# Mixer attention of a two-layer trunk: keys' 1/rms rows kept in four groups of 32 partitions and spread in two rounds

## The chip, the core and the metric

The kernel runs on one core of a Trainium2 chip. The metric is the device time of one execution in microseconds (us), the median of several runs. Engines are named as in the profile: PE (TensorE, matmuls), PEld (its weight loads), DVE (VectorE), ACT (ScalarE), POOL (GpSimd) and SP (SyncE, which issues most DMAs).

## The reference, cut to what matters

Two layers, each a mixer block and a sparse expert block, on 272 tokens (16 meta tokens and 256) of width 1024. The mixer runs a gated convolution and an attention of 8 heads beside each other, and merges them by gates. Of the attention, this part matters here:

```
k = jnp.concatenate([k_nope, k_r], axis=-1)     # 8 heads, 64 + 32 wide
q = _rmsnorm(q, q_norm_g)
k = _rmsnorm(k, k_norm_g)                       # k * rsqrt(mean(k*k) + eps) * g, per token and head
...
s = jnp.einsum('bqhd,bkhd->bhqk', qs, k) * scale
...
p = jax.nn.softmax(s, axis=-1)
```

Each head's keys are divided by their own root mean square, one number per token and head: 8 rows of 272 numbers.

## The kernel before, in words

Everything is fp32, with features on partitions and tokens along the free dimension. `hT` holds the hidden state as 8 tiles of 128 features by 272 tokens. A matmul with a weight tile of 1024 by 128 is eight accumulated matmuls of 128 by 128 by 272: `ztile` takes the next weight tile from a ring of four 1 MB buffers (`wraw`, filled by SP), multiplies it with `xg` and leaves the sum in one of three PSUM buffers `z`. In the second layer only 256 tokens are needed from the gates on, so those tiles have 256 columns.

The order of the work is written out by hand. The mixer is a loop over weight tiles: first the projections to queries and keys, then four pairs of tiles for the convolution input (`za`, `zb`), then 16 gate tiles. `attention()` is a generator, and the loops call it a step at a time, so that its small matmuls stand between the tiles' on PE. Each `yield` ends a step. A pair of convolution tiles has four steps (two behind `za`, two behind `zb`) and a gate tile has two. Between the steps, `taps()` puts convolution taps on DVE (`conv`) and on ACT and POOL (`conv2`).

The keys' norm goes like this. Sums of squares of all heads are collected in one PSUM tile, combined into `ss`, and transposed to tokens on partitions (`pt`, L403). DVE copies 16 numbers a token into `xr` (8 for queries, 8 for keys) and takes 1/rms into `rr` by three Newton steps (`rsqrt_steps`, L168 to L173). Two steps later PE transposes the keys' 8 columns back into 8 rows (`pk`, L419), and ACT copies them to `rk` (a tile of the name `mq`). Two steps later still, each head's row is spread over all 128 partitions by a matmul with a selector `seln[:, h]` (8 by 128, ones in row h), into one of the five PSUM banks of the name `aps`. DVE multiplies the head's keys by it (`kh`, L427). Four heads make one step, the other four the next. Scores, softmax, transposes and the mix with the values follow, one stage a weight tile; their PSUM tiles come from the same five banks `aps`.

At the start of a layer, DVE builds `seln` from the identity matrix (L243), clears the edge of `upad` and makes `gqk`. All matmuls go through the helper `mm` at L56, so the profile tells them apart by the tiles' names: `z<-xg,wraw` is a weight tile, `aps<-mq,seln` a spread.

Of the kernel before, what the change touches and what calls it, by code (L numbers as in the profile page):

```python
# [7 lines left out]
F32 = mybir.dt.float32  # L8
# [4 lines left out]
AF = mybir.ActivationFunctionType  # L13
# [7 lines left out]
T = 272  # L21
NH = 8
# [25 lines left out]
def trunk_kernel(ctx: ExitStack, tc: tile.TileContext, a: dict, out: bass.AP, dbg=None, stop=None):  # L48
    nc = tc.nc
    V, S, G, PE = nc.vector, nc.scalar, nc.gpsimd, nc.tensor  # L50
# [4 lines left out]
    def mm(o, l, r, start, stop):  # L55
        PE.matmul(o, l, r, start=start, stop=stop, skip_group_check=True)  # L56
# [57 lines left out]
    ident = pp.tile([128, 128], F32, name="ident")  # L114
# [36 lines left out]
    def rsqrt(pool, x, shape, y):  # L151
        run_all(rsqrt_steps(pool, x, shape, y))
        return y

    def run_all(g):
        for _ in g:
            pass

    def rsqrt_steps(pool, x, shape, y):

        w = pool.tile([128, T], F32, name="rq_w")
        n = 1
        for s_ in shape[1:]:
            n *= s_
        w = w[:, :n]
        if len(shape) == 3:
            w = w.rearrange("p (a b) -> p a b", a=shape[1])
        V.tensor_scalar(w.bitcast(I32), x.bitcast(I32), 1, None, op0=OP.logical_shift_right)  # L168
        V.tensor_scalar(y.bitcast(I32), w.bitcast(I32), -1.0, float(0x5f3759df), op0=OP.mult, op1=OP.add)
        for _ in range(3):  # L170
            V.scalar_tensor_tensor(w, y, -0.5, y, op0=OP.mult, op1=OP.mult)
            V.tensor_tensor(w, w, x, op=OP.mult)  # L172
            V.scalar_tensor_tensor(y, w, 1.5, y, op0=OP.add, op1=OP.mult)  # L173
            yield
# [8 lines left out]
    def square(sq, c, c0):  # L183

        S.activation(sq[:, c, c0:], hT[:, c, c0:], AF.Square)
        if c:
            V.tensor_add(sq[:, 0, c0:], sq[:, 0, c0:], sq[:, c, c0:])

    carry = None
    for l in range(NL):  # L190
# [22 lines left out]
        def big(tag, shape, dt=F32):  # L213
            t_ = mp.tile([128, 8 * T], F32, name=tag, tag=tag)
            n = 1
            for s_ in shape:
                n *= s_
            v_ = t_[:, :n]
            if dt != F32:
                v_ = v_.bitcast(dt)  # L220
            if len(shape) == 2:
                return v_.rearrange("p (a b) -> p a b", a=shape[0])
            if len(shape) == 3:
                return v_.rearrange("p (a b c) -> p a b c", a=shape[0], b=shape[1])
            return v_
# [4 lines left out]
        wuv = mp.tile([128, 512], F32, name="wuv")  # L230
        qh, kh = pp.tile([128, 8, T], F32, name="xh"), mp.tile([128, 8, T], F32, name="kh")
        rope = mp.tile([128, T], F32, name="rope")
        seln = mp.tile([8, 8, 128], F32, name="seln")
        upad = mp.tile([128, 4, T + KW - 1], F32, name="upad")
        gqk = mp.tile([64, 1], F32, name="gqk")

# [3 lines left out]
            scaled(xg, l, c, C_MIX, 0)  # L240
        for c in range(8):
            square(sq, c, 0)
        V.tensor_copy(seln, ident[0:8, 0:8, None].to_broadcast([8, 8, 128]))  # L243
        V.memset(upad[:, :, 0:KW - 1], 0.0)
        V.tensor_mul(gqk, cl[0:64, C_QN:C_QN + 1], cl[0:64, C_KN:C_KN + 1])
        if carry:
# [1 line left out]
        else:  # L248

            p = zp.tile([128, 512], F32, name="z", bufs=3)  # L250
# [13 lines left out]
        def ztile(c0, x=None):  # L264
            x = xg if x is None else x
            n = T - c0
            w_ = next_w()
            p = zp.tile([128, 512], F32, name="z", bufs=3)
            for c in range(8):
                mm(p[:, :n], w_[:, c * 128:(c + 1) * 128], x[:, c, c0:], c == 0, c == 7)  # L270
            return p[:, :n]
# [20 lines left out]
        def aps():  # L292
            return ap_.tile([128, 512], F32, name="aps", bufs=5)
# [16 lines left out]
        def attention():  # L310
# [8 lines left out]
            mq = mp.tile([128, T], F32, name="mq")  # L319
# [55 lines left out]
            for p in range(4):  # L375
                pk = aps()
# [29 lines left out]
            for i0, i1, n in ((0, 2, 128), (2, 3, 16)):  # L406
# [3 lines left out]
                V.tensor_copy(d_[:, :, 0], s_[:, :, :, 0:2])  # L410
                V.tensor_copy(k_[:, :, 1], s_[:, :, :, 8:10])
            rr = rsqrt(mp, xr, [128, 48], mp.tile([128, 48], F32, name="rr"))
            sc = mp.tile([128, 3, 8], F32, name="sc")
            V.tensor_scalar(sc, rr.rearrange("p (i x) -> p i x", i=3)[:, :, 0:8], SCALE, None, op0=OP.mult)
            yield
            yield
            pk = aps()
            for i, (q0, n) in enumerate(QT):
                PE.transpose(pk[0:8, q0:q0 + n], rr[:n, i * 16 + 8:i * 16 + 16], ident[:n, :n])  # L419
            rk = mp.tile([16, T], F32, name="mq")[0:8]  # L420
            S.activation(rk, pk[0:8, :T], AF.Copy)
            yield
            yield
            for h in range(NH):
                pb = aps()
                mm(pb[:, :T], seln[:, h], rk, True, True)
                V.tensor_mul(kh[0:96, h], kh[0:96, h], pb[0:96, :T])  # L427
                if h == 3:
                    yield
            yield  # L430
            oo = big("sq", [4, T])
            vt["o"] = oo
            PR, TP = {}, {}
# [114 lines left out]
            for x in range(11):  # L548
                p = x // 2
# [128 lines left out]
        V.tensor_mul(zk2[64:128], z[64:128], rs[64:128])  # L678
        V.tensor_add(zkr[64:128], zkr[64:128], zk2[64:128])
        att = attention()  # L680
        cvp = conv2()

# [81 lines left out]
        for i in range(8):  # L764
            p = ztile(t0, xh)
# [651 lines left out]
```

## Time and profile before

| | |
|---|---|
| median of 3 runs | 1758.39 us (1755.1 to 1759.44) |
| profiled execution, its own time | 1755.68 us |
| its span, first to last instruction | 1753.9 us |
| mean granted clock of TensorE | 0.995 |
| DMA | 559.38 MB, mean 319 GB/s |
| spreading matmuls `aps<-mq,seln`, both layers | 32 records, 9.2 us busy |
| keys' transposes (L419), both layers | 6 records |

A matmul in fp32 leaves two records. A row of the timeline gives the start and the length of a run of like instructions, in us from the span's start; in square brackets stands how long the engine sat idle before it and what ended that. PE's matmuls overlap in part, so the time that a run takes of PE's sequence is read from its start to the next run's start. "Granted clock" is the share of full speed at which TensorE was allowed to run, 1.00 being full.

### The profile page before, as it was taken

The page shows a single profiled execution, that of the slowest core. Times are in us where ns is not written, and L with a number is a line of the kernel's source. Part 1 is how long each engine was busy: PE and PEld are TensorE (multiplying, and loading weights), DVE is VectorE, ACT ScalarE, POOL GpSimd, SP SyncE. Part 2 cuts the span into 40 slices and gives each one's busy share as a digit, 9 for nine tenths or more (in the row PEclk, how much of TensorE's full clock was granted, in tenths as well). Part 3 has the DMA queues.
Part 4 walks back from the last instruction along what each step waited for, and adds up shares of the span by engine and source line. Part 5 has one row for each costly group of instructions (what it writes and reads, how often), then busy time and mean ns, then how long its engine had stood idle before and what let it go on. Part 6 is the DMA issues. An engine that isn't in the chain of part 4 may idle for free.

```text
span 1753.9 us, 29518 instructions
## 1 busy us (share of the span) xinstructions
PE 1729.5 (99%) x11611; PEld 1614.6 (92%) x11611; DVE 1108.9 (63%) x2900; ACT 480.9 (27%) x1480; POOL 335.5 (19%) x392
## 2 busy tenths in 40 slices
PE   9999999999999999999999999999999999999998
PEld 7678888999999999999986888899999999999998
DVE  5587369897888644444446883697888885333332
ACT  3443113345544111000024431133355441000000
POOL 0131012222111232232200210112221112212220
PEclk9999999999999999999999999999999999999999
DMA  6223456999999999999962234679999999999995
GB/s 235 73 97 121 168 193 240 384 375 420 420 420 421 420 418 419 421 420 417 417 256 81 92 126 167 222 281 394 372 424 424 423 417 417 397 371 397 398 393 206
DMA packets 80811, 559.38 MB, mean 319 GB/s; under 512 B 9240, under 2 KB 12248, under 8 KB 13208
## 3 DMA queue, kind: packets, MB, share of 16 engines
q1 hardware_dynamic: 49488, 338.54, 49.1%
q0 software_dynamic: 30464, 218.35, 30.5%
q8 instruction: 91, 1.49, 0.3%
q10 hardware_dynamic: 720, 0.60, 0.1%
q14 instruction: 48, 0.39, 0.1%
HBM read 556.18 MB, written 1.05 MB: 318 GB/s over the span
## 4 chain that ended last, share of the span: by engine, by line
PE 72%; DMA 10%; issue 9%; DVE 6%; POOL 2%; ACT 1%; SPq 0%; POOLq 0%; DVEq 0%; ACTq 0%
PE po L56 27%; PE z L56 22%; PE A L56 16%; DMA wraw<-vn 6%; DMA gb<-uv,iww 4%; PE aps L56 4%; POOL gb L1183 2%; PE wp L56 1%; DVE va L1194 1%; DVE gb L1208 1%; PE sc L56 1%; PE xp L56 0%; DMA wraw<-w_in 0%; DVE rq_w L172 0%; DVE ex L907 0%
## 5 line engine op out<-in xcount | busy, mean ns | idle before, releaser
L56 PE MATMUL A<-xh,wraw 128*128 128x160 f32 x3776 | 534.8, 301 | 1.2 <-ACT idxT L821 1.2
L56 PEld LDWEIGHTS A<-xh,wraw 128*128 128x128 f32 x3776 | 517.8, 191 | 1.6 <-issue 1.6
L1208 DVE SCALAR_TENSOR_TENSOR gb<-gb,xr 128x1024 f32<-128x1024 f32 x208 | 254.5, 1224 | 396.1 <-DMA gb<-uv,iww 395.5
L1183 POOL DMA_INDIRECT gb<-uv,iww x208 | 231.2, 1111 | 531.5 <-DVE va L1194 372.2
L56 PE MATMUL z<-xg,wraw 128*128 128x272 f32 (+2 forms) x1408 | 331.6, 393 | 0.2 <-DMA wraw<-w_in 0.2
L56 PEld LDWEIGHTS z<-xg,wraw 128*128 128x128 f32 (+1 forms) x1408 | 261.9, 191 | 55.0 <-issue 8.0
L56 PE MATMUL po<-Xh,wraw 128*128 128x160 f32 x2080 | 287.4, 300 | 3.8 <-DMA wraw<-vn 3.2
L56 PEld LDWEIGHTS po<-Xh,wraw 128*128 128x128 f32 x2080 | 283.2, 190 | 6.9 <-DMA wraw<-vn 5.6
L56 PE MATMUL po<-X,wraw 128*128 128x160 f32 x2016 | 278.4, 301 | 4.8 <-ACT gl L1243 2.5
L56 PEld LDWEIGHTS po<-X,wraw 128*128 128x128 f32 x2016 | 275.8, 191 | 6.8 <-DMA wraw<-vn 3.7
L1194 DVE SCALAR_TENSOR_TENSOR va<-gb,am,va 128x1024 f32<-128x1024 f32 x203 | 260.0, 1281 | 2.8 <-ACT am L1219 2.6
L1218 ACT ACTIVATE am<-am 128x1 f32<-128x1 f32 x208 | 41.3, 199 | 594.1 <-DVE gb L1208 594.0
L1122 ACT ACTIVATE ohA<-ohE,wlo 128x128 f16<-128x128 f16 x320 | 105.2, 429 | 6.3 <-DVE ohE L1119 5.5
L612 POOL TENSOR_TENSOR acc<-acc,cp 128x272 f32<-128x272 f32 (+1 forms) x60 | 50.6, 843 | 241.1 <-ACT cp L611 238.7
L1182 POOL COPY warm<-wraw 1x1 f32<-1x1 f32 x86 | 32.6, 379 | 319.7 <-DMA wraw<-vn 319.7
L604 DVE SCALAR_TENSOR_TENSOR acc<-upad,cols,acc 128x272 f32<-128x272 f32 (+1 forms) x180 | 88.6, 548 | 0.2
L1219 ACT ACTIVATE am<-am,iww 128x1 f32<-128x1 f32 x208 | 61.3, 295 | 6.9
L1119 DVE TENSOR_TENSOR ohE<-ioh,idxT 128x512 f16<-128x512 f16 x160 | 60.3, 419 | 0.0
L1133 ACT ACTIVATE Xh<-wp 128x260 f32<-128x260 f32 (+18 forms) x80 | 25.0, 312 | 124.9 <-DVE Xh L1130 114.9
L56 PE MATMUL z<-xh,wraw 128*128 128x272 f32 (+1 forms) x256 | 57.3, 386 | 0.0
L56 PEld LDWEIGHTS z<-xh,wraw 128*128 128x128 f32 x256 | 48.7, 190 | 8.2
L56 PE MATMUL wp<-ohE,ohA 128*128 128x128 f16 x640 | 51.0, 219 | 1.2 <-DVE ohA L1120 1.1
(311 smaller groups left out, 1381.0 us busy)
## 6 DMA issues: line engine op xcount, KB each, us to landing
wraw<-vn SPq DMA_DIRECT2D x128, 1024.0 KB, 10.8
wraw<-u SPq DMA_DIRECT2D x118, 1024.0 KB, 10.2
wraw<-w_in SPq DMA_DIRECT2D x27, 1024.0 KB, 4.9
wraw<-wq SPq DMA_DIRECT2D x16, 1024.0 KB, 4.8
we<-u SPq DMA_DIRECT2D x10, 1024.0 KB, 7.5
wraw<-w_out SPq DMA_DIRECT2D x8, 1024.0 KB, 4.8
wraw<-w_mla SPq DMA_DIRECT2D x4, 1024.0 KB, 4.7
wraw<-w_conv SPq DMA_DIRECT2D x4, 1024.0 KB, 5.1
```

Of the source, the lines that this page charges most:

```text
L56: PE.matmul(o, l, r, start=start, stop=stop, skip_group_check=True)
L604: V.scalar_tensor_tensor(acc[:, c, t0:], u_, weight(c, k), acc[:, c, t0:], op0=OP.mult, op1=OP.add)
L612: G.tensor_tensor(acc[:, 0, t0:], acc[:, 0, t0:], u_[:, t0:], op=OP.add)
L1119: V.tensor_tensor(E[q], ioh[:, None].to_broadcast(full), pairs(q, b), op=OP.is_equal)
L1122: S.activation(A_[1][:, t // 2, :, t % 2], E[0][:, t // 2, :, t % 2], AF.Copy, scale=wlo[:, 4 * b + t:4 * b + t + 1])
L1133: S.activation(x_, p[:, :, a:b].rearrange("p t j -> p j t"), AF.Copy, scale=1.0 / WS)
L1182: G.tensor_copy(warm[0:1], state["w"][0:1, 0:1])
L1183: G.indirect_dma_start(out=g_, out_offset=None, in_=a[f"uv{l}"], in_offset=bass.IndirectOffsetOnAxis(ap=iww[i].bitcast(I32)[:, m // 16, 0, ...
L1194: V.scalar_tensor_tensor(vac[i], r, m_, vac[i], op0=OP.mult, op1=OP.add)
L1208: V.scalar_tensor_tensor(u_, u_, 1.0, xrs[i], op0=OP.mult, op1=OP.mult, accum_out=m_)
L1218: S.activation(m_, m_, AF.Gelu_apprx_tanh)
L1219: S.activation(m_, m_, AF.Copy, scale=iww[i][:, m // 16, 1, m % 16:m % 16 + 1])
```

## The change

The keys' 1/rms numbers are laid out differently. Before their transpose, two DVE copies put them into `rw`, a tile of 128 columns for each block of tokens that is zero elsewhere: head `4 b + g` goes to column `32 g + b`. The transposes (L428 now) then give 128 rows, of which rows 32 g and 32 g + 1 hold two heads for each of the four groups g. `seln` becomes a tile with two rows in each group of 32 partitions, and each spreading matmul works on two rows of one group, so that the four matmuls of a round use four separate groups of rows. A round is four matmuls into four `aps` banks, then four multiplies of `kh`.

Two more `yield`s stand before the transposes, and two behind the first round; the one behind the last spread is gone. One weight tile (two steps) more lies between the end of the 1/rms chain and the transposes, and one weight tile stands between the two rounds.

```diff
-        seln = mp.tile([8, 8, 128], F32, name="seln")
+        seln = mp.tile([128, 2, 128], F32, name="seln")
+        rw = mp.tile([128, 3, 128], F32, name="rw")
...
-        V.tensor_copy(seln, ident[0:8, 0:8, None].to_broadcast([8, 8, 128]))
+        for g in range(4):
+            g_ = slice(32 * g, 32 * g + 2)
+            V.tensor_copy(seln[g_], ident[g_, 32 * g:32 * g + 2, None].to_broadcast([2, 2, 128]))
+        V.memset(rw, 0.0)
...
+            for i0, i1, n in ((0, 2, 128), (2, 3, 16)):
+                V.tensor_copy(rw[:n, i0:i1].rearrange("p i (g x) -> p i x g", g=4)[:, :, 0:2],
+                              rr[:n].rearrange("p (i q b g) -> p i q b g", i=3, q=2, b=2)[:, i0:i1, 1])
...
             yield
             yield
+            yield
+            yield
             pk = aps()
             for i, (q0, n) in enumerate(QT):
-                PE.transpose(pk[0:8, q0:q0 + n], rr[:n, i * 16 + 8:i * 16 + 16], ident[:n, :n])
-            rk = mp.tile([16, T], F32, name="mq")[0:8]
-            S.activation(rk, pk[0:8, :T], AF.Copy)
-            yield
-            yield
-            for h in range(NH):
-                pb = aps()
-                mm(pb[:, :T], seln[:, h], rk, True, True)
-                V.tensor_mul(kh[0:96, h], kh[0:96, h], pb[0:96, :T])
-                if h == 3:
+                PE.transpose(pk[:, q0:q0 + n], rw[:n, i], ident[:n, :n])
+            rk = mp.tile([128, T], F32, name="mq")
+            S.activation(rk, pk[:, :T], AF.Copy)
+            yield
+            yield
+            for b in range(2):
+                pbs = [aps() for _ in range(4)]
+                for g in range(4):
+                    g_ = slice(32 * g, 32 * g + 2)
+                    mm(pbs[g][:, :T], seln[g_, b], rk[g_], True, True)
+                for g in range(4):
+                    h = 4 * b + g
+                    V.tensor_mul(kh[0:96, h], kh[0:96, h], pbs[g][0:96, :T])
+                if b == 0:
                     yield
-            yield
+                    yield
```

On PE, from the transposes of `ss` to the first scores of layer 0, the order before is this (a row is a line of the program, the operation, output and inputs, the size, and how many in a row):

```order
L403 MATMUL aps<-ident,ss 128x128 x2
L403 MATMUL aps<-ident,ss 16x128
L56 MATMUL z<-xg,wraw 128x272 x8
L419 MATMUL aps<-ident,rr 8x128 x2
L419 MATMUL aps<-ident,rr 8x16
L56 MATMUL z<-xg,wraw 128x272 x8
L56 MATMUL aps<-mq,seln 128x272 x8
L56 MATMUL z<-xg,wraw 128x272 x8
L56 MATMUL aps<-kh,xh 128x144
```

And the same place of the changed program:

```order
L407 MATMUL aps<-ident,ss 128x128 x2
L407 MATMUL aps<-ident,ss 16x128
L56 MATMUL z<-xg,wraw 128x272 x16
L428 MATMUL aps<-ident,rw 128x128 x2
L428 MATMUL aps<-ident,rw 128x16
L56 MATMUL z<-xg,wraw 128x272 x8
L56 MATMUL aps<-mq,seln 128x272 x4
L56 MATMUL z<-xg,wraw 128x272 x8
L56 MATMUL aps<-mq,seln 128x272 x4
L56 MATMUL aps<-kh,xh 128x144
```

Two weight tiles instead of one now stand ahead of the keys' transposes, the spread is in two parts with a tile between, and the first scores come one tile later, straight behind the second part.

On DVE, from the last convolution pair to the first softmax of layer 0, the order before (`bz`, `az` and `upad` belong to that pair, `acc` rows are convolution taps, `g_...` is a gate tile's multiply, `kh` the keys' multiply, `mx` the softmax's maxima):

```order
L698 TENSOR_TENSOR bz<-z,rq_ym 128x272
L699 TENSOR_TENSOR az<-z,rq_ym 128x272
L427 TENSOR_TENSOR kh<-kh,aps 96x272 x4
L702 TENSOR_TENSOR upad<-az,bz 128x272
L602 TENSOR_SCALAR acc<-upad,cols_61 128x272
L604 SCALAR_TENSOR_TENSOR acc<-upad,cols_61,acc 128x272 x3
L427 TENSOR_TENSOR kh<-kh,aps 96x272 x4
L718 TENSOR_TENSOR g_623<-z,rq_ym 128x272
L604 SCALAR_TENSOR_TENSOR acc<-upad,cols_61,acc 128x272
L450 TENSOR_REDUCE mx<-aps 128x1 x4
```

And now:

```order
L711 TENSOR_TENSOR bz<-z,rq_ym 128x272
L712 TENSOR_TENSOR az<-z,rq_ym 128x272
L715 TENSOR_TENSOR upad<-az,bz 128x272
L615 TENSOR_SCALAR acc<-upad,cols_61 128x272
L617 SCALAR_TENSOR_TENSOR acc<-upad,cols_61,acc 128x272 x3
L731 TENSOR_TENSOR g_606<-z,rq_ym 128x272
L440 TENSOR_TENSOR kh<-kh,aps 96x272 x4
L617 SCALAR_TENSOR_TENSOR acc<-upad,cols_61,acc 128x272 x2
L731 TENSOR_TENSOR g_606<-z,rq_ym 128x272
L440 TENSOR_TENSOR kh<-kh,aps 96x272 x4
L617 SCALAR_TENSOR_TENSOR acc<-upad,cols_61,acc 128x272
L463 TENSOR_REDUCE mx<-aps 128x1 x4
```

The first four multiplies of `kh` stand behind the first gate tile's multiply and the second four behind the second's, and the first softmax comes a gate tile later. The second layer has the same differences with gate tiles of 256 columns. SP's DMAs and POOL's instructions stand in the order of before.

## The prediction

> **What bounds the kernel now.** I read the page first, for which engine is full.
>
> ```profile
> PE 1729.5 (99%) x11611; PEld 1614.6 (92%) x11611; DVE 1108.9 (63%) x2900; ACT 480.9 (27%) x1480; POOL 335.5 (19%) x392
> ```
>
> PE has work for 99% of the span, so a change gains only what it takes off PE's own sequence: a wait, a slow stretch, or matmuls. The view of waits, for PE over the whole span, has one line on the code that the diff touches:
>
> ```profile
> PE aps L419 <- DVE rr L173: 2.1, 2, 1.1
> ```
>
> Twice, once a layer, the keys' transposes wait for the end of the 1/rms chain on DVE, 2.1 us in all. The timeline of PE comes next, layer 0 first (start, length, how many records; each fp32 matmul leaves two records):
>
> ```profile
> 63.56 0.49 PE L403 MATMUL aps<-ident,ss 128*128 128x128 f32 x3
> 63.89 3.83 PE L56 MATMUL z<-xg,wraw 128*128 128x272 f32 x16
> 68.79 0.48 PE L419 MATMUL aps<-ident,rr 128*8 128x128 f32 x3 [1.07 <-DVE rr L173]
> 69.20 3.94 PE L56 MATMUL z<-xg,wraw 128*128 128x272 f32 x16
> 73.07 5.32 PE L56 MATMUL aps<-mq,seln 8*128 8x272 f32 x16
> 78.31 5.88 PE L56 MATMUL z<-xg,wraw 128*128 128x272 f32 x16
> 84.03 1.57 PE L56 MATMUL aps<-kh,xh 98*128 98x144 f32 x8
> 85.44 3.83 PE L56 MATMUL z<-xg,wraw 128*128 128x272 f32 x16
> 89.20 0.56 PE L56 MATMUL aps<-kh,xh 98*16 98x16 f32 x16
> ```
>
> From start to start, the eight spreading matmuls (seln) take 78.31 - 73.07 = 5.24 us and the weight tile behind them 84.03 - 78.31 = 5.72, though the next tile of the same shape takes 89.20 - 85.44 = 3.76. Layer 1, where a gate tile has 256 columns:
>
> ```profile
> 962.05 3.93 PE L56 MATMUL aps<-mq,seln 8*128 8x272 f32 x16
> 965.91 5.41 PE L56 MATMUL z<-xg,wraw 128*128 128x256 f32 x16
> 971.16 1.57 PE L56 MATMUL aps<-kh,xh 98*128 98x144 f32 x8
> 972.57 7.07 PE L56 MATMUL z<-xg,wraw 128*128 128x256 f32 x32
> 979.47 1.57 PE L56 MATMUL aps<-kh,xh 98*128 98x144 f32 x8
> ```
>
> Here the spread takes 3.86 and the tile behind it 5.25, against 6.90 / 2 = 3.45 for a later tile. The windows tell why (stretch, its length, busy time of PE, PEld, DVE, ACT and POOL with counts, granted clock, DMA):
>
> ```profile
> 73.00:75.00 2.00, 2.00 (x9) 1.59 (x9) 1.80 (x5) 1.29 (x4) 0.30 (x1) 1.00 0.39 66
> 75.00:77.00 2.00, 2.00 (x7) 1.54 (x6) 1.91 (x5) 1.66 (x2) 1.84 (x3) 0.61 0.95 401
> 77.00:79.00 2.00, 2.00 (x6) 1.06 (x5) 1.93 (x4) 0.00 (x0) 0.44 (x1) 0.50 0.14 57
> 79.00:81.00 2.00, 2.00 (x6) 1.54 (x5) 1.20 (x4) 0.00 (x0) 0.00 (x0) 0.50 0.03 8
> 81.00:83.00 2.00, 2.00 (x7) 1.54 (x7) 0.00 (x0) 0.00 (x0) 0.00 (x0) 0.68 0.00 0
> ...
> 966.00:968.00 2.00, 2.00 (x6) 1.62 (x7) 1.93 (x5) 0.00 (x0) 0.36 (x1) 0.58 0.12 49
> 968.00:970.00 2.00, 2.00 (x7) 1.62 (x6) 1.07 (x4) 0.00 (x0) 0.00 (x0) 0.56 0.00 0
> ```
>
> PE is busy in every one of these microseconds, yet the clock goes to 0.50. With one step between 1.00 and 0.50 in each window, the 0.61 puts the fall at 75.44, 2.37 us after the first spreading matmul; the 0.68 puts the end at about 82.3. In layer 1 it falls at 966.32, 4.27 us after the spread began, and is back by about 969.8. The lost time is (1 - clock) x 2 us a window: 2 x (0.39 + 0.50 + 0.50 + 0.32) = 3.42 in layer 0 and 2 x (0.42 + 0.44) = 1.72 in layer 1, 5.14 together. What the slow stretches have in common is a run of matmuls that use 8 of 128 rows.
>
> [...]
>
> **The change part by part.** *Transposes one tile later.* PE takes the second half of the last convolution pair (69.20) straight after the first half. The chain ends at 68.7, its two added copies and all; the earliest that PE can now ask is 69.20 - 0.41 - 1.07 + 3.87 = 71.6, with 3.87 the tile's own time (69.20 to 73.07). The wait of 2.1 us goes, with 2.9 us to spare. What is late next: nothing on PE, because the spread comes another tile later still. The transposes now load 128 weight columns instead of 8; the row at 63.56 is that form, three in 0.33 us against 0.41 for today's three, so I cost this at nothing.
>
> *The clock.* No run of eight-row matmuls is left that is long enough, if the cause is the one above: each round is short and followed by a whole tile or by scores on 98 rows. Gain 5.14; zero if the cause is another.
>
> *Four groups.* Take the lost clock and one normal tile out of the two spans: layer 0 leaves 10.96 - 3.42 - 3.76 = 3.78 for eight matmuls, layer 1 9.11 - 1.72 - 3.45 = 3.94. Sixteen take 7.72, 0.48 each, 1.93 for four in sequence. A round of four on separate rows of the array is nowhere in the trace. The nearest rows have matmuls on separate columns:
>
> ```profile
> 40.03 0.64 PE L56 MATMUL aps<-sqq,strip 96*16 96x272 f32 x4
> 40.60 3.94 PE L56 MATMUL z<-xg,wraw 128*128 128x272 f32 x16
> ...
> 240.28 0.43 PE L56 MATMUL scm<-uk,qm 128*32 128x128 f32 x8
> 240.64 0.73 PE L56 MATMUL z<-xg,wraw 128*128 128x272 f32 x2
> ```
>
> Two strip matmuls in two column groups take 0.57 instead of 0.96. Four scm matmuls in four groups take 0.36; at the 0.11 a record of the 128-column transposes (63.56 to 63.89, three) eight would take 0.88, so they run 2.4 times faster. That gives 1.93 / 2.4 = 0.80 a round. But a row group keeps 128-wide weight loads, and if these go one at a time at 0.11, eight records need 0.88. I take 0.9, by the weight loads, because the row at 63.56 is the nearest one with loads as wide as these. Ends: 0.48 (perfect overlap) and 1.93 (none); a loss beyond that would need a slower matmul, for which no row speaks. Four rounds at 0.9 are 3.6: gain 4.1, between 5.8 and 0.
>
> [...]
>
> *DVE and ACT.* These rows carry the cover:
>
> ```profile
> 16.07 0.68 DVE L243 COPY seln<-ident 8x1024 f32<-8x1024 f32 x1
> ...
> 19.12 0.44 DVE L305 TENSOR_SCALAR x<-aps 128x272 f32<-128x272 f32 x1 [2.24 <-PE aps L56]
> ...
> 64.71 0.18 DVE L410 COPY xr<-aps 128x16 f32<-128x16 f32 x1
> ...
> 69.78 2.56 DVE L604 SCALAR_TENSOR_TENSOR acc<-upad,cols,acc 128x272 f32<-128x272 f32 x6
> 73.17 0.44 DVE L698 TENSOR_TENSOR bz<-z,rq_ym 128x272 f32<-128x272 f32 x1 [0.83 <-PE z L56]
> ...
> 73.88 1.75 DVE L427 TENSOR_TENSOR kh<-kh,aps 96x272 f32<-96x272 f32 x4
> 75.56 0.43 DVE L702 TENSOR_TENSOR upad<-az,bz 128x272 f32<-128x272 f32 x1
> 76.02 0.74 DVE L602 TENSOR_SCALAR acc<-upad,cols 128x272 f32<-128x272 f32 x1
> ...
> 78.73 1.47 DVE L427 TENSOR_TENSOR kh<-kh,aps 96x272 f32<-96x272 f32 x4
> ...
> 84.23 0.44 DVE L718 TENSOR_TENSOR g<-z,rq_ym 128x272 f32<-128x272 f32 x1 [4.03 <-PE z L56]
> ```
>
> Four small selector copies and a memset replace one copy of 0.68: even at 0.68 for each of the five, 2.7 us more, only about 0.5 us would stick out of the 2.24 us of idle time behind it; copies of the small form take 0.18, so I cost it at nothing. The two copies into rw, at most 0.18 each, delay the taps behind them by 0.4.
>
> The second round reuses PSUM banks of the first, so PE waits there if DVE has not multiplied the first four heads. DVE's queue ahead of that: taps until 72.34 + 0.4 = 72.7, then the pair bz and az (73.88 - 73.17 = 0.71), upad (0.46), four taps (78.73 - 76.02 = 2.71), the gate's multiply (0.44) and four head multiplies (75.56 - 73.88 = 1.68): done at 78.7. PE reaches the second round at 71.6 + 0.41 + 3.76 + 0.9 + 3.76 = 80.4. The margin is 1.7 us; without it the gain shrinks by what DVE is late. Attention ends one tile later, and the convolution feeds the layer norm in the same place:
>
> ```profile
> 150.91 0.49 DVE L604 SCALAR_TENSOR_TENSOR acc<-upad,cols,acc 128x272 f32<-128x272 f32 x1
> ...
> 153.62 2.00 PE L56 MATMUL aps<-acc,ones 128*128 128x272 f32 x8
> ```
>
> The last tap ends at 151.4, 2.2 us before PE sums acc. DVE has the same work in 6.5 us less (layer 0's share of the gain: 1.07 + 10.96 - 3.76 - 1.8), and the idle 4.03 at 84.23 and these 2.2 cover 6.2 of that; the idle 0.83 at 73.17 covers the rest. No DMA and no POOL instruction changes place.
>
> **The sum.** 2.1 + 5.1 + 4.1 = 11.3 us. The profiled execution took 1755.68, so 1744.4 on its scale. It lies 2.7 under the median of the runs shown, 1758.39 (1755.1 to 1759.44); on the median's scale the forecast is 1747.1.
>
> **The rivals,** on the median's scale.
>
> *The clock falls as before.* If the fall hangs on something that stays, the 5.14 stays lost: gain 6.2, 1752.2. [...] Against it: both layers fall during or just behind the spread, and only the 1.07 us wait, which goes too, is another candidate.
>
> *The groups do not overlap.* Rounds of 1.93: gain 2.1 + 5.1 = 7.2, 1751.2. For it: no row of this form; against it: separate columns overlap.
>
> *DVE is late.* The margins of 1.7 and 2.2 us fail by 2 us a layer: gain 7.3, 1751.1. Against it: DVE's idle time after 84.03.
>
> *Slower.* Two rows a group are fewer than eight, and each round might itself pull the clock down for two windows, as layer 0's spread does, 3.42 us lost each. Four rounds lose 13.7 in place of 5.14; with nothing gained in sequence but the wait, this is 13.7 - 5.1 - 2.1 = 6.5 us slower, 1764.9. It decides where a round lasts as long as the 2.37 us that were enough in layer 0. Unoverlapped rounds come near that with 1.93; overlapped ones do not.
>
> *The first two together:* gain 2.1, 1756.3, no change that shows.
>
> **How the numbers follow.** About 0.3%, 5.3 us, is what a measurement of this kernel tells from no change. Chances: forecast 0.66, clock as before 0.08, no overlap 0.08, DVE late 0.04; these four are faster, 0.86. First two together 0.09: same. Slower 0.05. The range goes up to 1753, above the three faster rivals, and leaves out the 0.14 beyond; down to 1743, below the 1745.4 of perfect overlap by part of the 3.3 us by which the shown runs scatter under their median.
>
> **What would show it.** In the new trace: no wait before the transposes from rw; a clock of 1.00 through both rounds and the tile behind; each round 0.6 to 1.0 us from start to start; the tile behind it at 3.76 (3.45 in layer 1); no wait of PE on kh or acc. A clock of 0.50 near a round, a round near 1.9, or PE waiting on the kh multiplies would make the prediction wrong, by the rival that names it.

## The result, and the profile after

The changed kernel takes 1746.37 us (median of 4 runs, 1745.65 to 1746.77), the kernel before 1757.72 in the same comparison (1755.1 to 1759.44). The ratio is 0.9937, 95% interval 0.9921 to 0.9952: 11 us less. The profiled execution took 1746.77 us, with a span of 1745.0 and a mean granted clock of 0.998.

PE's timeline after the change, layer 0 and then the sums that the layer norm needs (start, length, records):

```profile
63.21 0.49 PE L407 MATMUL aps<-ident,ss 128*128 128x128 f32 x3
63.54 7.50 PE L56 MATMUL z<-xg,wraw 128*128 128x272 f32 x32
70.87 0.54 PE L428 MATMUL aps<-ident,rw 128*128 128x128 f32 x3
71.35 3.94 PE L56 MATMUL z<-xg,wraw 128*128 128x272 f32 x16
75.21 0.74 PE L56 MATMUL aps<-mq,seln 2*128 2x272 f32 x8
75.88 3.93 PE L56 MATMUL z<-xg,wraw 128*128 128x272 f32 x16
79.75 0.74 PE L56 MATMUL aps<-mq,seln 2*128 2x272 f32 x8
80.42 1.67 PE L56 MATMUL aps<-kh,xh 98*128 98x144 f32 x8
...
146.44 2.00 PE L56 MATMUL aps<-acc,ones 128*128 128x272 f32 x8
```

No idle time stands before the transposes (70.87). A round takes 75.88 - 75.21 = 0.67 us, the tile between the rounds 79.75 - 75.88 = 3.87. Layer 1 has the same rounds, 0.67 and 0.68:

```profile
960.62 0.74 PE L56 MATMUL aps<-mq,seln 2*128 2x272 f32 x8
961.29 3.72 PE L56 MATMUL z<-xg,wraw 128*128 128x256 f32 x16
964.94 0.74 PE L56 MATMUL aps<-mq,seln 2*128 2x272 f32 x8
965.62 1.68 PE L56 MATMUL aps<-kh,xh 98*128 98x144 f32 x8
```

The windows over the spread of layer 0 (busy times, then granted clock, DMA share and GB/s) show the clock at 1.00, where the kernel before was down to 0.50:

```profile
74.00:76.00 2.00, 2.00 (x15) 1.17 (x14) 1.93 (x3) 1.98 (x5) 1.84 (x3) 1.00 0.58 246
76.00:78.00 2.00, 2.00 (x9) 1.69 (x10) 2.00 (x5) 0.65 (x1) 1.84 (x3) 1.00 0.03 8
78.00:80.00 2.00, 2.00 (x12) 1.41 (x15) 1.45 (x5) 0.00 (x0) 0.48 (x1) 1.00 0.00 0
80.00:82.00 2.00, 2.00 (x17) 1.48 (x14) 1.79 (x6) 0.00 (x0) 0.00 (x0) 1.00 0.63 123
```

DVE keeps ahead of PE at both places where it could have been late:

```profile
77.01 1.46 DVE L440 TENSOR_TENSOR kh<-kh,aps 96x272 f32<-96x272 f32 x4
...
80.50 1.48 DVE L440 TENSOR_TENSOR kh<-kh,aps 96x272 f32<-96x272 f32 x4 [0.21 <-PE aps L56]
...
143.33 0.49 DVE L617 SCALAR_TENSOR_TENSOR acc<-upad,cols,acc 128x272 f32<-128x272 f32 x1
```

It has multiplied the first four heads at 78.5, 1.3 us before PE starts the second round, and waits for that round itself. The last convolution tap ends at 143.8, 2.6 us before PE sums `acc` at 146.44.

From the transposes of `ss` to those sums, the same work on both sides, layer 0 took 153.62 - 63.56 = 90.06 us and takes 146.44 - 63.21 = 83.23. Layer 1 took 83.20 and takes 78.09; its first and last rows, before and then after:

```profile
952.62 0.49 PE L403 MATMUL aps<-ident,ss 128*128 128x128 f32 x3
...
1035.82 1.89 PE L56 MATMUL aps<-acc,ones 128*128 128x256 f32 x8
```

```profile
948.84 0.49 PE L407 MATMUL aps<-ident,ss 128*128 128x128 f32 x3
...
1026.93 1.89 PE L56 MATMUL aps<-acc,ones 128*128 128x256 f32 x8
```

The mixers are thus 6.83 + 5.11 = 11.9 us shorter, while the two profiled executions differ by only 8.9. The largest of PE's waits that grew is far from the change, in the expert block. The first line is the kernel before, the second the changed one:

```profile
PE wp L56 <- DVE ohA L1120: 1.1, 2, 0.6
PE wp L56 <- DVE ohA L1133: 5.7, 3, 2.7
```

It is 4.6 us longer, and some other waits are shorter. Whether it belongs to the change is asked below.

### The profile page after: what moved, and what is told of

Same layout as the page of the kernel before. It is cut to its first block, busy times and chain, and to the rows that moved or that the text cites. A ratio compares the mean times of both kernels' runs of the same rounds, so it can differ in the third digit from the quotient of the medians.

```text
span 1745.0 us, 29536 instructions
## 1 busy us (share of the span) xinstructions
PE 1719.9 (99%) x11611; PEld 1605.7 (92%) x11611; DVE 1110.3 (64%) x2912; ACT 480.3 (28%) x1480; POOL 351.8 (20%) x392
## 4 chain that ended last, share of the span: by engine, by line
PE 71%; DMA 11%; issue 9%; DVE 5%; POOL 2%; ACT 1%; SPq 0%; POOLq 0%; DVEq 0%; ACTq 0%
PE po L56 26%; PE z L56 23%; PE A L56 16%; DMA wraw<-vn 7%; DMA gb<-uv,iww 4%; PE aps L56 3%; POOL gb L1196 2%; PE wp L56 1%; DVE va L1207 1%; DVE gb L1221 1%; PE sc L56 1%; PE xp L56 0%; DMA wraw<-w_in 0%; DVE ex L920 0%; DVE tkw L806 0%
## 5 line engine op out<-in xcount | busy, mean ns | idle before, releaser
L1196 POOL DMA_INDIRECT gb<-uv,iww x208 | 235.4, 1132 | 525.9 <-DVE va L1207 381.5
L56 PE MATMUL z<-xg,wraw 128*128 128x272 f32 (+2 forms) x1408 | 327.8, 390 | 0.2 <-DMA wraw<-w_in 0.2
L1195 POOL COPY warm<-wraw 1x1 f32<-1x1 f32 x86 | 40.8, 475 | 316.4 <-DMA wraw<-vn 316.3
L625 POOL TENSOR_TENSOR acc<-acc,cp 128x272 f32<-128x272 f32 (+1 forms) x60 | 54.1, 902 | 228.2 <-ACT cp L624 219.3
```

Of the source, the lines that this page charges most:

```text
L625: G.tensor_tensor(acc[:, 0, t0:], acc[:, 0, t0:], u_[:, t0:], op=OP.add)
L1195: G.tensor_copy(warm[0:1], state["w"][0:1, 0:1])
L1196: G.indirect_dma_start(out=g_, out_offset=None, in_=a[f"uv{l}"], in_offset=bass.IndirectOffsetOnAxis(ap=iww[i].bitcast(I32)[:, m // 16, 0, ...
```

## The experiments

My theory had three parts: the wait before the transposes (2.1 us), a clock that halves because few of the array's rows are in use for too long (5.1), and the overlap of four matmuls on separate rows (4.1). The chief rival was that the clock fell for another reason, the wait above all. All ratios are against runs of the kernel before on the same chip. Every variant computes the whole reference.

**Transposes later, alone.**

```diff
             yield
             yield
+            yield
+            yield
             pk = aps()
```

> The kernel before with two more yields ahead of the transposes, nothing else. [...] Rival (the clock falls because of the idle 1.07 us): clock 1.00 throughout the spread, each spread 3.9 us from start to start, time 7 us under.

Measured: ratio 0.9988 (0.9976 to 0.9999), 2.1 us less. PE's wait before the transposes is gone, and the clock falls all the same:

```profile
75.75 3.93 PE L56 MATMUL aps<-mq,seln 8*128 8x272 f32 x16
79.61 5.62 PE L56 MATMUL z<-xg,wraw 128*128 128x272 f32 x16
85.06 1.57 PE L56 MATMUL aps<-kh,xh 98*128 98x144 f32 x8
```

```profile
78.00:80.00 2.00, 2.00 (x10) 1.37 (x9) 2.00 (x7) 0.00 (x0) 0.66 (x1) 0.97 0.00 0
80.00:82.00 2.00, 2.00 (x6) 1.54 (x5) 1.16 (x4) 0.00 (x0) 0.00 (x0) 0.50 0.04 8
```

The fall comes at 79.9 (the 0.97 of the first window puts it there), behind 4.1 us of spreading with PE never idle. In layer 1 the spread takes 5.42 us and the tile behind it 5.33, where a later tile takes 3.46: the clock falls there too. The gain is about what the wait lasted, not the 7 us of the rival, though its interval nearly reaches no change; the wait is not the cause of the fall.

**The same spread on 128 rows.** The keys' numbers are copied into columns 0 to 7 of `rw`, which is zero elsewhere, so the added rows of the spread data are zero, and those of the selector are too; place, count and order of the spread stay. Cut to the tiles and the transposes:

```diff
-        seln = mp.tile([8, 8, 128], F32, name="seln")
+        seln = mp.tile([128, 8, 128], F32, name="seln")
+        rw = mp.tile([128, 3, 128], F32, name="rw")
...
-                PE.transpose(pk[0:8, q0:q0 + n], rr[:n, i * 16 + 8:i * 16 + 16], ident[:n, :n])
-            rk = mp.tile([16, T], F32, name="mq")[0:8]
+                PE.transpose(pk[:, q0:q0 + n], rw[:n, i], ident[:n, :n])
+            rk = mp.tile([128, T], F32, name="mq")
...
```

> The kernel before, with its eight spreading matmuls contracting over all 128 rows instead of 8: rows 8 to 127 of the selector and of the spread rows are zero. Same place, same wait of 1 us a layer, same count. Theory (few active rows lower the clock): clock 1.00 through the spread, each spread 3.9 us, no slow tile behind it, time 5 us under the kernel before. Rival (the wait, or the place, lowers it): clock 0.50 as before, time within 1 us of before. If rows that hold zeros count as inactive, it also falls as before.

Measured: 0.9967 (0.9957 to 0.9977), 5.8 us less, though the wait before the transposes grew to 2.7 us. PE in layer 0, and the windows:

```profile
72.92 3.83 PE L56 MATMUL aps<-mq,seln 128*128 128x272 f32 x16
76.58 3.83 PE L56 MATMUL z<-xg,wraw 128*128 128x272 f32 x16
80.25 1.57 PE L56 MATMUL aps<-kh,xh 98*128 98x144 f32 x8
```

```profile
74.00:76.00 2.00, 2.00 (x10) 1.65 (x10) 1.95 (x6) 1.98 (x5) 1.28 (x2) 1.00 0.87 283
76.00:78.00 2.00, 2.00 (x11) 1.65 (x10) 1.93 (x3) 0.62 (x1) 1.12 (x2) 1.00 0.57 242
```

These are eight matmuls one after another, as long as before, with slightly more idle time ahead of the transposes. Of the spread only the rows differ, and the clock stays at 1.00 in both layers (from 72 to 82 us and from 961 to 969). The mean clock of all eight executions is 0.998 or 0.999, against 0.993 to 0.998 in the kernel before. That settles the cause in this kernel: with 8 rows in use the clock went to 0.50, with 128 it stayed at 1.00, though 120 of them held zeros.

**32 and 64 rows,** the same edit with tiles of that height.

> The kernel before with its eight spreading matmuls on 32 rows (24 of them zero) instead of 8. [...]

> The same on 64 rows. [...]

Measured: 32 rows 1.0006 (0.9995 to 1.0018), 64 rows 0.9976 (0.9964 to 0.9988). With 32 rows, layer 0:

```profile
73.39 4.96 PE L56 MATMUL aps<-mq,seln 32*128 32x272 f32 x16
78.27 6.24 PE L56 MATMUL z<-xg,wraw 128*128 128x272 f32 x16
84.35 1.57 PE L56 MATMUL aps<-kh,xh 98*128 98x144 f32 x8
```

```profile
76.00:78.00 2.00, 2.00 (x6) 1.20 (x4) 1.93 (x3) 0.99 (x1) 1.68 (x2) 0.53 0.74 311
```

With 64 rows:

```profile
73.51 3.93 PE L56 MATMUL aps<-mq,seln 64*128 64x272 f32 x16
77.37 3.93 PE L56 MATMUL z<-xg,wraw 128*128 128x272 f32 x16
81.14 1.57 PE L56 MATMUL aps<-kh,xh 98*128 98x144 f32 x8
```

With 32 rows the clock did not stay up in layer 0 (0.50 from 78 to 82 us); in layer 1 of the same profile spread and tile took 3.86 and 3.56 us, which shows no fall. With 64 rows it was 1.00 in layer 0 from 70 to 86 us, and layer 1 has the same 3.86 and 3.56. Both kernels had the longer wait of this layout, 2.7 us. Those 0.6 us more can account for most of what the gain with 64 rows, 4.2 us, lacks of the 5.1 at which the clock was priced.

**A tile between two halves of the 8-row spread,** without groups; first with the transposes in their old place, then with them a tile later.

```diff
                 if h == 3:
                     yield
-            yield
+                    yield
```

> The kernel before with a weight tile between the first four and the last four 8-row spreads; no groups, transposes where they were. Theory with the 2.37 us that were enough in layer 0: each half is 1.9 us, too short, clock 1.00, time 5 us under the kernel before, with the 2.1 us wait still there. Rival (any run of 8-row matmuls near 2 us is enough, as in my slower case): clock falls at one or both halves, time between 2 under and 5 over.

> The changed kernel without the groups: 8-row spreads one after another, four and four with a weight tile between, transposes a tile later. Theory: no wait, clock 1.00, each round 1.9 us; time 7 us under the kernel before, the sum of wait and clock, and 4 to 5 us over the changed kernel. Rival (the clock falls at 1.9 us rounds): gain 2 us or less.

Measured: 0.9991 (0.9979 to 1.0004) and 0.9967 (0.9954 to 0.9980), 1.6 and 5.8 us less. The first is no difference that can be told, where I had expected 5 us. Its own profiled execution shows no fall in the mixers: the clock is 1.00 from 72 to 84 us, and in layer 1 the tile between the halves takes 3.65 us, as between the rounds of the changed kernel. But the mean clock of its 12 timed executions runs from 0.996 to 0.999, and those at 0.999 are the short ones (1751.5 to 1753.6 us, against 1755.4 to 1759.6 at 0.996 and 0.997). So the clock falls more in some executions than in others; the mean does not tell where. The second kernel gains less than the expected 7, and its profile has a fall in layer 0, behind the second half:

```profile
81.74 2.10 PE L56 MATMUL aps<-mq,seln 8*128 8x272 f32 x8
83.77 1.84 PE L56 MATMUL aps<-kh,xh 98*128 98x144 f32 x8
85.41 5.39 PE L56 MATMUL z<-xg,wraw 128*128 128x272 f32 x16
90.73 0.56 PE L56 MATMUL aps<-kh,xh 98*16 98x16 f32 x16
```

```profile
84.00:86.00 2.00, 2.00 (x10) 1.66 (x10) 1.73 (x6) 0.00 (x0) 0.00 (x0) 0.78 0.98 414
```

Halves of 2.03 us (83.77 - 81.74), with scores on 98 rows behind them, still came with a fall here (0.50 from 86 to 88 us). With the move and the split but no groups the gain is 5.8 us; the changed kernel, run beside it, gained 12.

**The groups alone:** both rounds back to back, transposes in the old place.

```diff
-            yield
-            yield
             pk = aps()
...
                 if b == 0:
                     yield
-                    yield
+            yield
```

> The changed kernel without both moves: four groups, both rounds back to back, transposes where they were. Overlap as in the changed kernel: first round 0.67 us. The second round needs the banks of the first, and so waits for DVE's multiplies of four heads, 1 to 2 us of PE idle in each layer. The 2.1 us wait stays. Clock: spread and wait together near 3 us with little array work, so it may fall in a layer; theory says it falls at most as in layer 1 of before (1.7 us). Time 3 to 7 us under the kernel before. Rival (the split brings nothing): no PE wait between the rounds, time 9 us under.

Measured: 0.9970 (0.9959 to 0.9982), 5.3 us less. Layer 0:

```profile
73.14 2.71 PE L56 MATMUL aps<-mq,seln 2*128 2x272 f32 x16
75.78 5.62 PE L56 MATMUL z<-xg,wraw 128*128 128x272 f32 x16
81.24 1.57 PE L56 MATMUL aps<-kh,xh 98*128 98x144 f32 x8
```

The two rounds take 2.64 us, where apart they take 1.34. The second stands in the wait for DVE's multiplies, which free its banks. The tile of weights between the rounds hides that, 1.3 us a layer. The tile behind took 5.46 instead of 3.76: the clock fell here too (0.50 from 78 to 80 us). In layer 1 that tile took 3.56, which shows no fall. So the split is worth something, but I had put the idle part too high: it is 1.1 us in both layers together. The rest, 0.75 us a layer (2.64 - 1.34 - 0.55), I put down to matmuls that go one by one as DVE's multiplies, 0.37 us each, free the banks; that is an estimate, and no view shows it.

**The changed kernel with the transposes in the old place.**

```diff
-            yield
-            yield
             pk = aps()
```

> The changed kernel with the transposes where they were: four groups, weight tile between the rounds, attention not shifted. Theory: the wait of about 1.0 to 1.5 us a layer is back, now longer by the two copies into rw (0.2 us); the rest of the gain stays; time 9 us under the kernel before, 2 to 2.5 us over the changed kernel. Rival (the move is worth nothing, the wait is hidden elsewhere): same as the changed kernel.

Measured: 0.9950 (0.9934 to 0.9966), 8.8 us less, 1747.67 against 1745.94 of the changed kernel, run beside it. PE's waits:

```profile
PE aps L426 <- DVE sc L421: 2.5, 2, 1.3
```

The wait is back and a little longer. As the medians stand, the move is worth 1.7 us, near the 2 to 2.5 expected; the intervals overlap. The mixers alone show more: 85.06 + 79.88 = 164.9 us in this profile against 161.3 in the changed kernel's, 3.6 longer. The waits are 2.5 of that. The rest is in part the scores behind the second round, which take 1.86 us to the next tile instead of 1.51 in layer 0, because DVE's multiplies come later there. A shorter wait in the expert block, 1.6 us here, hides part of this in the total.

**Both kernels again,** unchanged.

> The kernel before once more, unchanged, for a second profile and more times. Its runs spread from 1755.1 to 1759.44. [...] Ratio 1.000.

> The changed kernel once more, for a second profile. In the first one PE's wait for DVE ohA in the peer stage of layer 0 was 5.7 us against 1.1 before, which took 3.3 us of the mixer's gain back. If that comes from the change, it is here again, and a profile of the kernel before has about 1 us of it; if it is chance, it differs from execution to execution. Time 11 us under the kernel before.

Measured: 1.0001 (0.9991 to 1.0010) and 0.9931 (0.9916 to 0.9946). The kernel before, in layer 1 this time:

```profile
964.85 5.21 PE L56 MATMUL aps<-mq,seln 8*128 8x272 f32 x16
969.99 5.77 PE L56 MATMUL z<-xg,wraw 128*128 128x256 f32 x16
975.60 1.57 PE L56 MATMUL aps<-kh,xh 98*128 98x144 f32 x8
```

Spread and tile take 10.75 us here against 9.11 in the first profile: the slow stretch is twice as long, about 6.8 us by the windows (967.4 to 974.2) against 3.4 (966.3 to 969.8). The cost of the clock in the mixers of the kernel before is thus an estimated 5.1 us in one execution and 6.8 in another. The two mixers take 174.9 us in this profile of the kernel before and 161.3 in the second one of the changed kernel, 13.6 less. The second profile of each kernel also has the wait in the expert block:

```profile
PE wp L56 <- DVE ohA L1120: 3.5, 3, 1.8
```

```profile
PE wp L56 <- DVE ohA L1133: 5.4, 2, 3.9
```

The first of these is the kernel before, the second the changed one. Over all profiles the wait is 1.1 and 3.5 us before, 5.7 and 5.4 after, 6.3 with the later transposes alone, 5.5 with the two halves alone, 4.9 with the groups alone, 4.9, 2.3 and 4.7 on 32, 64 and 128 rows, and 6.5 with every spreading matmul twice (below). It is 1.6 and 0.9 in the kernels that have all of the change but the later transposes, and all but the groups. It follows no part of the change: it is long in kernels with one part each and short in two with most of it. What sets it stays open.

**Every spreading matmul twice,** one execution.

```diff
-                for g in range(4):
+                for g in (0, 1, 2, 3, 0, 1, 2, 3):
                     g_ = slice(32 * g, 32 * g + 2)
                     mm(pbs[g][:, :T], seln[g_, b], rk[g_], True, True)
```

> The changed kernel with every spreading matmul issued twice: eight matmuls in a round, the second four in the same order and to the same banks. A round of four took 0.67 us where perfect overlap would be 0.48. If the 0.19 is paid once a round, eight take 0.48 + 0.48 + 0.19 = 1.15; if it is paid for every four, 1.34; if the weight loads of 0.11 each bounded the round as I had assumed, eight would take 1.8.

Measured, a round of layer 0:

```profile
75.47 1.20 PE L56 MATMUL aps<-mq,seln 2*128 2x272 f32 x16
76.59 3.93 PE L56 MATMUL z<-xg,wraw 128*128 128x272 f32 x16
```

Eight take 1.12 us. Four more matmuls cost 1.12 - 0.67 = 0.45, no more than one alone (0.48); some 0.2 us (0.67 - 0.45) are paid once a round. Weight loads at 0.11 us each, one after another, do not bound it: the 16 records would need 1.8 us. The execution took 1749.4 us; one says nothing firm about the time.

No variant was measured faster than the changed kernel.

## Why the prediction was right, step by step

*The wait.* Predicted 2.1 us; 2.1 alone, 1.7 by the medians as the last step of the full change. Right, with nothing late behind it. One reading was off: the chain ends at 68.64 before its two added copies, and not with them. After the change the copies end at 68.57 and the transposes come at 70.87, so 2.3 us were to spare and not 2.9.

*The clock.* Predicted 5.14 from one execution. The 128-row spread gives 5.8 with a wait that is 0.6 longer, so an estimated 6.4 on average, in line with 5.1 and 6.8 in the two profiles. The cause is shown: with the spread on 8 rows the clock went to 0.50, on 128 rows it stayed at 1.00. PE was busy for all of these stretches (2.00 of every 2 us), so idleness is not what lowers the clock here. In the expert block it fell beside idle time of PE: in the first profile of the changed kernel PE waits 2.61 us until 395.75, and the clock is at 0.50 from 395.50 on; in the first profile of the kernel before it waits 2.01 us until 600.91, and the clock is at 0.50 from 601.10 on. The rival "the clock falls as before" did not come: over both rounds and the tiles behind them the clock is 1.00.

*The groups.* Predicted 0.9 us a round, measured 0.67. The term was mis-sized: I let the weight loads go one by one at 0.11 us, and the doubled round shows that they do not: its 16 records took 1.12 us and not 1.8. Overlap is worth 4 x (1.93 - 0.67) = 5.0 us and not 4.1. A round is thus 1.93 / 0.67 = 2.9 times as fast as the estimate for four in sequence.

*DVE.* Predicted 78.7 for the end of the first four multiplies and 80.4 for the second round; measured 78.5 and 79.75. The margin of 2.2 us before the layer norm became 2.6.

*The sum.* Predicted 11.3 us; the two mixers show 11.9, the medians 11.35. The two profiled executions differ by only 8.9, with a longer wait elsewhere that no experiment ties to a part of the change. That the medians meet the sum so closely is partly luck: the overlap is worth 0.9 more than I put down, the clock was priced from an execution with one short stretch (the second pair of profiles has the mixers 13.6 us apart), and in the first pair the rest of the program took some of the gain back.

*The slower rival's point of decision* was wrong, though the case did not come. I had said that a stretch must last 2.37 us; 2.03 us with 98-row scores behind it was enough in layer 0 of the halves with later transposes. Halves without groups can thus come with a fall, and the rounds of the changed kernel, with the clock at 1.00, did not. My rival of rounds that do not overlap had kept the whole 5.14 with rounds of 1.93 us, and that was wrong.

*Where the limit lies.* The runs show it case by case, each spread taken from its start to the next run's start. In layer 0 the clock fell to 0.50 with 8 rows in one piece (5.24 us, in part at the lower clock, and 3.86 with the later transposes), with 8 rows in halves of 2.03 us and later transposes, with 32 rows (4.88 us, also in part at the lower clock) and with the groups back to back (2.64 us). There it stayed at 1.00 with the halves alone, with 64 rows (3.86 us), with 128 rows (3.66 us) and with the changed kernel's rounds of 0.67 us. With 32 rows and with the groups back to back it fell in layer 0 and, by a tile of 3.56 us behind the spread, not in layer 1. What the clock follows between 8 rows and 64, and why one program falls in one layer or execution and not in another, was not shown.

## What to carry to other kernels

In the kernel before PE was busy all the time and still ran at a clock of 0.50 from 77 to 81 us: look at the granted clock over stretches of matmuls that use few rows, and count what it costs the tile behind them too (5.72 us instead of 3.76). Matmuls on few rows did best here on separate groups of 32 rows, in short rounds (0.67 us against an estimated 1.93 in sequence) between matmuls on all rows. A round here writes one PSUM bank for each group, four of the five, so other matmuls belong between two rounds while the first is read out.

## What the runs showed of the hardware that I had not expected

- Rows of zeros kept the clock up: with 120 of them added to the spread it stayed at 1.00, and the kernel was 5.8 us faster.
- Four fp32 matmuls of 272 columns on four row groups take 0.67 us, eight 1.12: four in about the time of one, and 0.2 us once.
- The same program loses 5.1 or 6.8 us to the clock in its mixers from one execution to the next, by estimates from two profiles: in layer 1 the slow stretch lasts about 3.4 us in the first and 6.8 in the second. That is 1.7 us of the 5.4 by which these two executions differ (1755.68 and 1761.04 us).
